# A two-layer recurrent trunk on one core: the SSD mixer's decays summed in PSUM, and a unit's preparation placed behind the unit before it

## The chip, the core and the metric

The kernel is one program on one core of a Trainium2 chip. The core has a matrix engine (TensorE; PE in the profile, with PEld for its weight loads), three engines for elementwise work (VectorE, ScalarE and GpSimd: DVE, ACT and POOL) and SyncE (SP), which issues transfers. Each engine works off its own instructions in the order in which they stand; engines wait for each other through semaphores. Matrix products are written to PSUM, eight banks of 128 x 512 float32.

The metric is the device time of the program in microseconds (us). The kernel before was timed in three runs.

## The reference, cut to what matters

A two-layer network takes 1024 prompt tokens and 8 separate decode tokens. Layer 0 is a hybrid mixer and an MLP; layer 1 is an SSD mixer and an MLP. The change is in the SSD mixer, whose core is a linear recurrence with one decay per head, evaluated in blocks of 128 tokens (chunks):

```python
def decay_linear_attention(q, k, v, g, s0, chunk):
    ...
    causal = (idx[:, None] >= idx[None, :])[None, :, :, None, None]
    def step(s, blk):
        qc, kc, vc, gc = blk
        gcum = jnp.cumsum(gc, axis=1)
        diff = gcum[:, :, None] - gcum[:, None, :]
        decay = jnp.where(causal, jnp.exp(jnp.where(causal, diff, 0.0)), 0.0)
        scores = jnp.einsum('bigk,bjgk->bijg', qc, kc)
        y_intra = jnp.einsum('bijgr,bjgrv->bigrv', scores[..., None] * decay, vc)
        y_inter = jnp.einsum('bigk,bgrkv->bigrv', qc, s) * jnp.exp(gcum)[..., None]
        g_end = gcum[:, -1]
        s_new = s * jnp.exp(g_end)[..., None, None] + jnp.einsum(
            'bjgk,bjgrv->bgrkv', kc, vc * jnp.exp(g_end[:, None] - gcum)[..., None])
        return s_new, y_intra + y_inter
```

There are 4 groups of 8 heads. `q` (C in the kernel), `k` (B) and so `scores` are shared by the 8 heads of a group; `decay`, a 128 x 128 matrix for every chunk and head, is not.

## The kernel before, in words

**Stages.** The tokens lie on the free axis (1032 columns, in three slices of 344), features on the 128 partitions. The residual stream is held as two exact float32r parts (`xh`, `xl`), weights are split likewise (`whi` by ACT on line 144, `wlo` by DVE on line 145), and each product of a projection is three matmuls of 344 columns (lines 150 to 152). A projection tile of 128 features is 72 of them, into three banks of the tag `g`.

**The SSD stage** (`ssm_mixers`) runs over the four groups. For each group `ssd_group` is a generator: it emits a piece of the recurrence and yields, and at every yield `ssm_mixers` emits one projection tile (`next(tiles)`): a tile of the next group's x, B or C with its convolution and silu (`conv_tile`, `conv_silu`; on DVE lines 1451, 409, 411, 413, 421), or a gate tile of the group before (`gate`, `gates`; lines 1476, 421, 1487). What is emitted is then put in order by a list scheduler with a timing model of its own: where it believes that TensorE would wait, it moves later projection matmuls forward. So the order on an engine differs from the order in the code, and is printed below where it matters.

**A unit** is two chunks; a group has four. In the kernel before each unit is emitted whole, then a projection tile, one or two steps of the decode recurrence (`ssd_decode`; DVE lines 1727 and 1731, POOL line 1730), and another tile. A unit is:

- preparation: x is transposed (line 1598) and scaled by dt to `xdt` (DVE, line 1600), and that to `xd2` (POOL, line 1602); B is transposed and the scores B C are made (lines 1610, 1611), then `bt` is copied (ACT, line 1612) and the causal mask put on the scores (`sc`, DVE, line 1613); for each pair of heads a bank gets the row term of the decay by two matmuls with 64 rows of contraction (line 1621, `sel` and `grow`), and ACT subtracts the column term with a Relu for each head and chunk (line 1625, 16 of 128 x 128) and takes two Exps of 128 x 1024 (line 1628); DVE multiplies one chunk's eight matrices by the scores and POOL the other's (line 1629); two more pairs of matmuls (line 1636) and two Exps (line 1637) give `EG`; ACT scales the skip term (line 1640);
- products, for each of the two chunks: `py` (line 1648, from `xdt` and `E`; added to x by DVE, line 1650), `pi` (line 1654, from the state; scaled by DVE, line 1657), and `pS` (line 1660, the new state; added by DVE, line 1666).

**PSUM.** Three banks serve the projections (`g`), three the tag `m` (`pm()`: the transposes, the scores, the decay terms, `EG`, the decode's broadcasts), two the tag `s` (`ps2()`: py, pi, pS). A matmul waits until the tile that had its bank has been read. In the trace the tiles are named `pg`, `pm` and `ps`.

Of the kernel before, what the change touches and what calls it, by code (L numbers as in the profile page):

```python
# [18 lines left out]
P = 128  # L19
T = 1032                     # 1024 prompt tokens, then 8 decode tokens  # L20
# [4 lines left out]
KT = 8                       # k-tiles of the model dimension  # L25
WN = 384                     # tokens of a group of a narrow projection
CH = 128                     # mixer chunk
# the tokens in nines of 128, the last of which overlaps
# [16 lines left out]
# order of the hybrid projection's m-tiles (first column of each)  # L45
# [14 lines left out]
# blocks of the output projections: the first packed column's k-tile, the mixer outputs  # L60
# [13 lines left out]
# columns of the retention's constants  # L74
# [9 lines left out]
class Pools:  # L84
    """A mixer's two pools: what the output projection's first block needs or reuses, and the rest."""
# [10 lines left out]
class Kern:  # L96
# [35 lines left out]
    def load_w(self, src, n, normw=None, lo_eng=None, dst=None, norm_eng=None):  # L132
        """src [128, n] of a packed weight unit -> exact float32r high and low parts."""
# [31 lines left out]
    def products(self, src, M, normw, pss):  # L165
        """The products of an m-tile over the model dimension; yields after every sixth."""
# [512 lines left out]
    def gdn_head(self, gp, h, feat, st):  # L679
# [10 lines left out]
        def bc(x, n=4):      # [128, n] -> [128, n, 128]  # L690
            return x.unsqueeze(2).to_broadcast([P, n, 128])
# [1194 lines left out]
```

## Time and profile before

| what | value |
|---|---|
| three runs | 3253.94, 3255.11, 3256.97 us |
| median | 3255.11 us |
| span of the profiled execution, first to last instruction | 3239.5 us |
| TensorE busy in the span | 3086.4 us (95%) |
| VectorE, GpSimd, ScalarE busy | 1740.3, 1241.3, 896.2 us |
| TensorE's clock over the span, share of full speed | 0.960 |

The profile gives the profiled execution's span, and no time of its own beside it; the median of the runs is 15.6 us above the span, which is what lies around it. TensorE is busy nearly always, but two things hide in that: it is busy for twice as long where its clock is at half, and a matmul's modelled end overlaps the next one's start, so that the time a matmul really takes in a stream is read from the starts. The rows below the diff show both for the stretch 1588 to 2262 us, which holds the SSD recurrence from the first unit's decay terms to the last group's products.

### The profile page before, as it was taken

The page shows a single profiled execution, that of the slowest core. Times are in us where ns is not written, and L with a number is a line of the kernel's source. Part 1 is how long each engine was busy: PE and PEld are TensorE (multiplying, and loading weights), DVE is VectorE, ACT ScalarE, POOL GpSimd, SP SyncE. Part 2 cuts the span into 40 slices and gives each one's busy share as a digit, 9 for nine tenths or more (in the row PEclk, how much of TensorE's full clock was granted, in tenths as well). Part 3 has the DMA queues.
Part 4 walks back from the last instruction along what each step waited for, and adds up shares of the span by engine and source line. Part 5 has one row for each costly group of instructions (what it writes and reads, how often), then busy time and mean ns, then how long its engine had stood idle before and what let it go on. Part 6 is the DMA issues. An engine that isn't in the chain of part 4 may idle for free. (4 is left out here: it accounts for less than half of the span.)

```text
span 3239.5 us, 49390 instructions
## 1 busy us (share of the span) xinstructions
PE 3086.4 (95%) x19566; PEld 2929.6 (90%) x19566; DVE 1740.3 (54%) x3201; ACT 896.2 (28%) x1828; POOL 1241.3 (38%) x1234
## 2 busy tenths in 40 slices
PE   7989998989999999999999999999899999999998
PEld 6888888879999999999987788887899999999998
DVE  7664667464333333337886785967635333333334
ACT  3222221223111111114444444354213111111112
POOL 4232324155333323225355555444625332332324
PEclk9899999889999999999998898998899999999999
DMA  3011103142111111111111111222431111111112
GB/s 123 20 47 54 47 26 112 55 168 64 46 46 47 49 46 46 48 48 40 55 56 58 69 62 43 82 69 79 157 140 43 46 47 49 46 46 50 46 46 72
DMA packets 102326, 202.13 MB, mean 62 GB/s; under 512 B 12624, under 2 KB 27728, under 8 KB 102096
## 3 DMA queue, kind: packets, MB, share of 16 engines
q1 hardware_dynamic: 94800, 173.82, 16.7%
q0 software_dynamic: 7296, 25.17, 2.0%
q8 instruction: 154, 2.52, 0.3%
q14 instruction: 76, 0.62, 0.1%
HBM read 157.94 MB, written 38.89 MB: 61 GB/s over the span
## 5 line engine op out<-in xcount | busy, mean ns | idle before, releaser
L150 PE MATMUL pg<-xh,whi 128*128 128x344 f32 x3072 | 1020.7, 332 | 10.2 <-DVE sxc L1451 6.5
L152 PE MATMUL pg<-xh,wlo 128*128 128x344 f32 x3072 | 1012.9, 330 | 2.8 <-DVE wlo L145 2.8
L151 PE MATMUL pg<-xl,whi 128*128 128x344 f32 x3072 | 1009.0, 328 | 0.0
L150 PEld LDWEIGHTS pg<-xh,whi 128*128 128x128 f32 x3072 | 593.0, 193 | 27.7 <-issue 8.8
L152 PEld LDWEIGHTS pg<-xh,wlo 128*128 128x128 f32 x3072 | 592.8, 193 | 12.7 <-issue 5.2
L144 ACT CAST whi<-raw 128x512 fp32r<-128x512 f32 (+2 forms) x443 | 271.0, 612 | 1191.5 <-PE pg L151 723.9
L151 PEld LDWEIGHTS pg<-xl,whi 128*128 128x128 f32 x3072 | 592.3, 193 | 8.8 <-issue 5.8
L140 POOL TENSOR_TENSOR raw<-raw,vec 128x512 f32<-128x512 f32 x264 | 300.7, 1139 | 589.9 <-DMA raw<-w 339.7
L151 PE MATMUL pg<-alo,whi 128*128 128x344 f32 (+2 forms) x1476 | 472.4, 320 | 0.0
L152 PE MATMUL pg<-ahi,wlo 128*128 128x344 f32 (+2 forms) x1476 | 472.3, 320 | 0.0
L150 PE MATMUL pg<-ahi,whi 128*128 128x344 f32 (+2 forms) x1476 | 471.6, 319 | 0.0
L1236 DVE TENSOR_TENSOR acc<-acc,pg 128x344 f32<-128x344 f32 x360 | 182.8, 511 | 385.4 <-PE pg L152 385.4
L145 POOL TENSOR_TENSOR wlo<-raw,whi 128x512 fp32r<-128x512 f32 (+2 forms) x179 | 223.7, 1251 | 327.7 <-ACT whi L144 326.6
L145 DVE TENSOR_TENSOR wlo<-raw,whi 128x512 fp32r<-128x512 f32 x264 | 209.6, 794 | 193.3 <-ACT whi L144 172.2
L1227 POOL TENSOR_TENSOR r<-r 128x344 f32<-128x344 f32 x192 | 145.9, 760 | 387.6 <-ACT ahi L1226 338.5
L152 PEld LDWEIGHTS pg<-ahi,wlo 128*128 128x128 f32 x1476 | 277.6, 188 | 0.0
L150 PEld LDWEIGHTS pg<-ahi,whi 128*128 128x128 f32 x1476 | 277.5, 188 | 0.0
L151 PEld LDWEIGHTS pg<-alo,whi 128*128 128x128 f32 x1476 | 277.3, 188 | 0.0
L1228 DVE TENSOR_TENSOR alo<-r,ahi 128x344 fp32r<-128x344 f32 x192 | 135.6, 707 | 253.8 <-POOL r L1227 253.8
L1226 ACT ACTIVATE ahi<-r 128x344 fp32r<-128x344 f32 x192 | 94.5, 492 | 338.5 <-DVE r L1225 338.5
L1225 DVE SCALAR_TENSOR_TENSOR r<-pg,rstd_bc 128x344 f32<-128x344 f32 x186 | 94.8, 510 | 76.9 <-PE pg L152 75.6
L150 PE MATMUL pg<-mhi,whi 128*128 128x344 f32 x408 | 131.3, 322 | 4.1 <-DVE acc L1342 4.1
(534 smaller groups left out, 4422.9 us busy)
## 6 DMA issues: line engine op xcount, KB each, us to landing
raw<-w SPq DMA_DIRECT2D x256, 256.0 KB, 2.6
raw<-wis SPq DMA_DIRECT2D x80, 256.0 KB, 2.6
raw<-wih SPq DMA_DIRECT2D x56, 256.0 KB, 2.6
mraw<-spill SPq DMA_DIRECT2D x17, 512.0 KB, 4.1
accd<-ost SPq DMA_DIRECT2D x48, 172.0 KB, 2.1
acc<-accd SPq DMA_DIRECT2D x16, 516.0 KB, 6.9
dS<-sstate SPq DMA_DIRECT2D x32, 256.0 KB, 3.5
o_sssm<-dS POOLq DMA_DIRECT2D x32, 256.0 KB, 2.4
```

The source lines that it names most:

```text
L140: (norm_eng or nc.gpsimd).tensor_tensor(out=r3, in0=r3, in1=normw.unsqueeze(2).to_broadcast([P, k, n // k]), op=ALU.mult)
L144: nc.scalar.copy(hi[:, :n], raw[:, :n])
L145: (lo_eng or nc.vector).tensor_tensor(out=lo[:, :n], in0=raw[:, :n], in1=hi[:, :n].bitcast(F32), op=ALU.subtract)
L150: t.matmul(ps, lhsT=whi, rhs=xhi, start=start, stop=False)
L151: t.matmul(ps, lhsT=whi, rhs=xlo, start=False, stop=False)
L152: t.matmul(ps, lhsT=wlo, rhs=xhi, start=False, stop=stop)
L1225: nc.vector.scalar_tensor_tensor(out=r, in0=ps, scalar=0.0, in1=self.rstd_bc[:, s], op0=ALU.max, op1=ALU.mult)
L1226: nc.scalar.activation(hi[:, s], r, AF.Square)
L1227: nc.gpsimd.tensor_tensor(out=r, in0=r, in1=r, op=ALU.mult)
L1228: nc.vector.tensor_tensor(out=lo[:, s], in0=r, in1=hi[:, s].bitcast(F32), op=ALU.subtract)
L1236: nc.vector.tensor_tensor(out=s, in0=s, in1=ps, op=ALU.add)
```

## The change

The decay matrices of two heads and both chunks of a unit are now built in one PSUM bank by five matmuls: the causal mask (a 128 x 128 matrix of 0 and -1e30 through an identity, 512 columns), the row term of each head (256 columns) and, for each chunk, minus the column term of both heads (256 columns, the moving operand a broadcast of `nsel`). One Exp of 128 x 512 then reads the bank. The 16 Relus and two Exps of a unit become four Exps, and the mask is no longer put on the scores: `bt` and `sc` become one copy `sb` on ACT. `E` is split by heads rather than by chunks, so that both chunks' products read both of its tiles. `grow`, `sel` and `selg` get 128 partitions (the upper 64 rows of `grow` are zero), so these matmuls contract over 128 rows in place of 64.

The preparation becomes a function. That of the first unit is emitted ahead of a yield of its own (ten yields for a group where there were nine), and that of unit u + 1 directly behind unit u's products, ahead of the next projection tile.

```diff
-        grow = gp.tile([64, SEQ], F32R, tag="row", name="sgrow", bufs=1)
+        grow = gp.tile([P, SEQ], F32R, tag="row", name="sgrow", bufs=1)
+        nc.vector.tensor_scalar(out=grow[64:].rearrange("p (c k) -> p c k", c=8), in0=self.U[64:].unsqueeze(1).to_broadcast([64, 8, 128]),
+                                scalar1=0.0, scalar2=None, op0=ALU.mult)
...
+        idr = gp.tile([P, P], F32R, name="sidr")
+        nc.vector.tensor_copy(idr, self.ident)
+        mmr = gp.tile([P, P], F32R, name="smmr")
+        nc.vector.tensor_copy(mmr, self.minmask)
+        nsel = gp.tile([P, 32], F32R, name="snsel")
+        nc.vector.tensor_scalar(out=nsel, in0=sel.bitcast(F32), scalar1=-1.0, scalar2=None, op0=ALU.mult)
...
-        for u in range(4):
+        def prepare(u):
...
+            E = [gp.tile([P, 4, 2, 128], F32, tag="E", name="E", bufs=2) for k in range(2)]
+            for hp in range(4):
+                h = g * 8 + hp * 2
+                pG = self.pm()
+                p4 = pG.rearrange("p (h c k) -> p h c k", h=2, c=2)
+                t.matmul(p4, lhsT=st["idr"], rhs=st["mmr"].unsqueeze(1).unsqueeze(1).to_broadcast([P, 2, 2, 128]), start=True, stop=False)
+                for k in range(2):
+                    t.matmul(p4[:, k], lhsT=st["sel"][:, h + k:h + k + 1].to_broadcast([P, P]),
+                             rhs=grow[:, ucols].rearrange("p (c k) -> p c k", c=2), start=False, stop=False)
+                for j in range(2):
+                    t.matmul(p4[:, :, j], lhsT=grow[:, (c0 + j) * 128:(c0 + j + 1) * 128],
+                             rhs=st["nsel"][:, h:h + 2].unsqueeze(2).to_broadcast([P, 2, 128]), start=False, stop=j == 1)
+                a.activation(E[hp // 2][:, hp % 2 * 2:hp % 2 * 2 + 2], p4, AF.Exp)
...
+            a.copy(sb, pt.rearrange("p (c k) -> p c k", c=4))
...
-            a.copy(bt, pt[:, 0:256].rearrange("p (c k) -> p c k", c=2))
-            v.tensor_tensor(out=sc, in0=pt[:, 256:512].rearrange("p (c k) -> p c k", c=2),
-                            in1=self.U.unsqueeze(1).to_broadcast([P, 2, 128]), op=ALU.mult)
...
-                        a.activation(E[j][:, hp * 2 + k, :], pG[:, k * 256 + j * 128:k * 256 + j * 128 + 128], AF.Relu,
-                                     scale=-1.0, bias=st["gc"][:, c0 + j, h:h + 1])
-            for j in range(2):
-                a.activation(E[j], E[j], AF.Exp, scale=-1.0)
-                (gs if j else v).tensor_tensor(out=E[j], in0=E[j], in1=sc[:, j, :].unsqueeze(1).to_broadcast([P, 8, 128]), op=ALU.mult)
+            for k in range(2):
+                (gs if k else v).tensor_tensor(out=E[k], in0=E[k], in1=sb[:, 2:4].unsqueeze(1).to_broadcast([P, 4, 2, 128]), op=ALU.mult)
...
+        unit = prepare(0)
+        yield
+        for u in range(4):
+            c0 = u * 2
+            E, sb, xdt, xd2, EG = unit
...
+            if u < 3:
+                unit = prepare(u + 1)
             yield
```

The rest of the diff takes comments away and changes no instruction.

**The order on TensorE** at the start of the second unit of the first group, as the kernel before has it: a projection tile ends (`pg`), the unit's x is transposed (line 1598), then B (1610) and the scores (1611), then come the decay terms (1621) with the next tile's projection between them.

```order
L152 MATMUL pg<-xh_78,wlo 128x344
L1598 MATMUL pm<-c_67,x 128x128 x8
L1610 MATMUL pm<-c_67,bc 128x128
L1611 MATMUL pm<-bc 128x128
L1610 MATMUL pm<-c_67,bc 128x128
L1611 MATMUL pm<-bc 128x128
L1621 MATMUL pm<-sgrow,ssel 128x256 x2
L150 MATMUL pg<-xh_71,whi 128x344
L151 MATMUL pg<-xl_79,whi 128x344
L1621 MATMUL pm<-sgrow,ssel 128x256 x2
```

In the changed kernel the same tile's end is followed by the unit's first products (1665 py, 1671 pi, 1677 pS) and the decay terms of the unit after it: 1609 the mask, 1611 the rows, 1614 the columns.

```order
L152 MATMUL pg<-xh_78,wlo 128x344
L1665 MATMUL ps<-E,xdt 64x128 x8
L1671 MATMUL ps<-bc,S 128x128 x4
L1609 MATMUL pm<-smmr,sidr 128x512
L1611 MATMUL pm<-sgrow,ssel 128x256
L1677 MATMUL ps<-xd_15432,sb 128x512
L1611 MATMUL pm<-sgrow,ssel 128x256
L1614 MATMUL pm<-snsel,sgrow 128x2x128 x2
L1609 MATMUL pm<-smmr,sidr 128x512
L1611 MATMUL pm<-sgrow,ssel 128x256 x2
L1614 MATMUL pm<-snsel,sgrow 128x2x128 x2
L1609 MATMUL pm<-smmr,sidr 128x512
```

Before, 38 projection matmuls of the next tile stood between the tile's end and the first products; now none does. Behind the rows shown come the rest of the third group of decay terms, 20 projection matmuls, the second chunk's products, the fourth group, the transposes, the scores and `EG`, and then 49 projection matmuls.

**The order on VectorE** at the same place, before: the tile's evictions (1451), the unit's `xdt` (1600) around the convolution's first row (409), the convolution (411, 413), and only then the masked scores (1613).

```order
L1451 TENSOR_TENSOR sxc<-pg,rstd_bc 128x344 x2
L1600 TENSOR_TENSOR xdt<-pm,dt 128x512
L409 TENSOR_SCALAR x<-sxc,scwh 128x8
L1600 TENSOR_TENSOR xdt<-pm,dt 128x512
L411 SCALAR_TENSOR_TENSOR x<-sxc,scwh,x 128x1024
L413 SCALAR_TENSOR_TENSOR x<-sst,scwh,x 128x8
L411 SCALAR_TENSOR_TENSOR x<-sxc,scwh,x 128x1024
L413 SCALAR_TENSOR_TENSOR x<-sst,scwh,x 128x8
L411 SCALAR_TENSOR_TENSOR x<-sxc,scwh,x 128x1024
L413 SCALAR_TENSOR_TENSOR x<-sst,scwh,x 128x8
L1613 TENSOR_TENSOR sc<-pm,c_67 128x256
```

In the changed kernel the same convolution stands between the readings of two product banks: py's (1667) and pi's (1674), with the decode's reductions (1750) ahead of it and a silu (421) behind.

```order
L409 TENSOR_SCALAR x<-sxc,scwh 128x8
L1667 TENSOR_TENSOR x<-x,ps 128x4x128
L1750 TENSOR_REDUCE dy<-dpr 128x4 x2
L411 SCALAR_TENSOR_TENSOR x<-sxc,scwh,x 128x1024
L413 SCALAR_TENSOR_TENSOR x<-sst,scwh,x 128x8
L411 SCALAR_TENSOR_TENSOR x<-sxc,scwh,x 128x1024
L413 SCALAR_TENSOR_TENSOR x<-sst,scwh,x 128x8
L411 SCALAR_TENSOR_TENSOR x<-sxc,scwh,x 128x1024
L413 SCALAR_TENSOR_TENSOR x<-sst,scwh,x 128x8
L1674 TENSOR_TENSOR yi<-ps,EG 128x512
L421 SCALAR_TENSOR_TENSOR x<-th,x 128x516
L1683 TENSOR_TENSOR S<-S,ps 128x512
```

So the convolution moved from behind the readers of the `m` banks to between the readers of the two `s` banks.

## Rows read from the trace of the kernel before

**Rows 1.** The windows view of the SSD stretch and of a stretch in the first MLP: length, then busy time (and instructions) of each engine, then the granted clock of TensorE as a share of full speed, the DMA share and GB/s.

```profile
1588.00:2262.00 674.00, 628.35 (x3751) 551.48 (x3750) 510.27 (x799) 310.42 (x721) 337.22 (x296) 0.91 0.19 64
1000.00:1100.00 100.00, 100.00 (x639) 100.00 (x638) 35.95 (x63) 17.95 (x32) 31.43 (x32) 1.00 0.16 48
```

**Rows 2.** TensorE's waits in the stretch 1588 to 2262 us, by line and by who ended them: us in total, times, the longest.

```profile
PE pm L1621 <- DVE xdt L1600: 14.0, 8, 3.0
PE pm L1621 <- DVE sc L1613: 13.0, 5, 3.4
PE pg L150 <- DVE sxc L1451: 6.5, 4, 2.7
PE pg L152 <- DVE wlo L145: 2.6, 3, 1.7
PE ps L1648 <- DVE x L1650: 2.2, 3, 1.0
PE pm L1636 <- ACT E L1625: 1.9, 2, 0.9
PE ps L1660 <- DVE x L1650: 1.7, 3, 0.7
PE pg L150 <- ACT whi L144: 1.3, 2, 0.7
PE ps L1654 <- DVE S L1666: 1.2, 3, 0.8
```

**Rows 3.** The timeline around one such wait, TensorE and then VectorE: start, us, the instruction with its count, and in brackets the idle time before it and who ended it.

```profile
1635.81 1.03 PE L1598 MATMUL pm<-c,x 128*128 128x128 f32 x8
...
1637.12 0.39 PE L1611 MATMUL pm<-bc 128*128 128x128 f32 x2
1640.23 0.50 PE L1621 MATMUL pm<-sgrow,ssel 64*128 64x256 f32 x2 [2.73 <-DVE xdt L1600]
...
1636.36 1.78 DVE L145 TENSOR_TENSOR wlo<-raw,whi 128x512 fp32r<-128x512 f32 x1
1638.06 0.67 DVE L1731 TENSOR_REDUCE dy<-dpr 128x4 f32<-128x512 f32 x1
...
1639.51 0.68 DVE L1600 TENSOR_TENSOR xdt<-pm,dt 128x512 f32<-128x512 f32 x1
```

**Rows 4.** The windows view around another of these waits, 2.2 us long and ended at 1713.8 us; the columns are those of rows 1.

```profile
1710.00:1714.00 4.00, 1.80 (x12) 1.55 (x11) 4.00 (x7) 1.25 (x2) 0.48 (x3) 0.96 0.13 37
1714.00:1730.00 16.00, 16.00 (x51) 13.40 (x52) 6.88 (x15) 9.46 (x24) 7.77 (x6) 0.50 0.11 35
1730.00:1741.00 11.00, 10.25 (x81) 8.10 (x79) 8.62 (x16) 1.98 (x5) 5.62 (x6) 0.97 0.06 25
```

**Rows 5.** TensorE's timeline where one pair of line 1621 stands between projection matmuls at full clock.

```profile
1590.10 0.32 PE L151 MATMUL pg<-xl,whi 128*128 128x344 f32 x1
1590.35 0.49 PE L1621 MATMUL pm<-sgrow,ssel 64*128 64x256 f32 x2
1590.78 0.43 PE L152 MATMUL pg<-xh,wlo 128*128 128x344 f32 x1
1591.04 0.32 PE L150 MATMUL pg<-xh,whi 128*128 128x344 f32 x1
```

**Rows 6.** ScalarE's groups in the stretch 1588 to 2262 us: busy us, mean ns of one, idle before and who ended it.

```profile
L1625 ACT ACTIVATE E<-pm,sgc 128x128 f32<-128x128 f32 x256 | 71.8, 373 | 59.1 <-PE pm L1621 58.9
...
L1628 ACT ACTIVATE E<-E 128x1024 f32<-128x1024 f32 x32 | 32.8, 1081 | 0.0
...
L1637 ACT ACTIVATE EG<-pm 128x512 f32<-128x512 f32 x32 | 18.0, 622 | 0.0
```

**Rows 7.** VectorE's groups in the same stretch, in the same columns.

```profile
L145 DVE TENSOR_TENSOR wlo<-raw,whi 128x512 fp32r<-128x512 f32 x64 | 65.8, 1029 | 12.9 <-PE pg L152 11.8 <-ACT whi L144 0.9
L411 DVE SCALAR_TENSOR_TENSOR x<-sxc,scwh,x 128x1024 f32<-128x1024 f32 x36 | 52.1, 1446 | 4.0 <-ACT x L408 3.8
...
L421 DVE SCALAR_TENSOR_TENSOR x<-th,x 128x516 f32<-128x516 f32 x24 | 23.3, 970 | 2.8 <-ACT th L420 2.8
...
L421 DVE SCALAR_TENSOR_TENSOR z<-th,z 128x516 f32<-128x516 f32 x28 | 22.4, 801 | 10.8 <-ACT th L420 10.8
L1629 DVE TENSOR_TENSOR E<-E,sc 128x1024 f32<-128x1024 f32 x16 | 21.9, 1370 | 15.8 <-ACT E L1628 15.8
L1650 DVE TENSOR_TENSOR x<-x,ps 128x512 f32<-128x512 f32 x32 | 21.8, 683 | 27.5 <-PE ps L1648 27.5
...
L1731 DVE TENSOR_REDUCE dy<-dpr 128x4 f32<-128x512 f32 x31 | 21.0, 676 | 4.1 <-POOL dpr L1730 4.1
...
L413 DVE SCALAR_TENSOR_TENSOR x<-sst,scwh,x 128x8 f32<-128x8 f32 x36 | 13.3, 370 | 0.3
```

**Rows 8.** TensorE's timeline over a chunk's products: py (two passes of eight), pi (two of four), pS (two of one), and the next projection matmul.

```profile
1605.89 1.09 PE L1648 MATMUL ps<-E,xdt 128*64 128x128 f32 x16 [0.60 <-DVE x L1650]
1606.91 1.16 PE L1654 MATMUL ps<-bc,S 128*128 128x128 f32 x8
1607.91 1.02 PE L1660 MATMUL ps<-xd,bt 128*128 128x512 f32 x2
1608.37 0.72 PE L152 MATMUL pg<-xh,wlo 128*128 128x344 f32 x1
```

**Rows 9.** VectorE's groups, in the columns of rows 7, in the stretch 1000 to 1100 us of the first MLP, the weights' low parts.

```profile
L145 DVE TENSOR_TENSOR wlo<-raw,whi 128x512 fp32r<-128x512 f32 x9 | 6.2, 690 | 13.7 <-ACT whi L144 13.4
```

More of the change, by code (lines that the diff above doesn't have):

```diff
@@ L1428, in ssm_setup @@
                 nc.tensor.transpose(pt[:64, j * 128:(j + 1) * 128], ghl[:, half * 4 + j, :], self.ident)
-            nc.scalar.copy(grow[:, half * 512:half * 512 + 512], pt[:64, :])
-        sel = gp.tile([64, 32], F32R, name="ssel")
-        nc.vector.tensor_tensor(out=sel, in0=self.ident[:64, 0:32], in1=self.ident[:64, 32:64], op=ALU.add)
+            nc.scalar.copy(grow[:64, half * 512:half * 512 + 512], pt[:64, :])
+        sel = gp.tile([P, 32], F32R, name="ssel")
+        nc.vector.tensor_tensor(out=sel, in0=self.ident[:, 0:32], in1=self.ident[:, 32:64], op=ALU.add)
+        idr = gp.tile([P, P], F32R, name="sidr")
[4 more added lines that the diff above has]
+        nc.vector.tensor_scalar(out=nsel, in0=sel.bitcast(F32), scalar1=-1.0, scalar2=None, op0=ALU.mult)
         pt = self.pm()
@@ L1437, in ssm_setup @@
         nc.scalar.copy(dg, pt[:32, 0:16])
-        st.update(dt=dt, gc=gc, kdf=kdf, egend=egend, grow=grow, sel=sel, sel8=sel8, dg=dg)
+        st.update(dt=dt, gc=gc, kdf=kdf, egend=egend, grow=grow, sel=sel, nsel=nsel, idr=idr, mmr=mmr, sel8=sel8, dg=dg)
         return st
@@ L1582, in v64 @@
             return ap.rearrange("p (h k) -> p h k", h=8)
-        selg = gp.tile([64, 8, 64], F32R, tag="selg", name="selg", bufs=1)
-        v.tensor_copy(selg, st["sel"][:, hs].bitcast(F32).unsqueeze(2).to_broadcast([64, 8, 64]))
+        selg = gp.tile([P, 8, 64], F32R, tag="selg", name="selg", bufs=1)
+        v.tensor_copy(selg, st["sel"][:, hs].bitcast(F32).unsqueeze(2).to_broadcast([P, 8, 64]))
         selg = selg.rearrange("p h k -> p (h k)")
         dec = self.ssd_decode(gp, g, x, B, C, st, half, selg)
-        S = None
-        for u in range(4):
+        grow = st["grow"]
+        def prepare(u):
             c0 = u * 2
             ucols = slice(c0 * 128, c0 * 128 + 256)
+            E = [gp.tile([P, 4, 2, 128], F32, tag="E", name="E", bufs=2) for k in range(2)]
[11 more added lines that the diff above has]
+                a.activation(E[hp // 2][:, hp % 2 * 2:hp % 2 * 2 + 2], p4, AF.Exp)
+            pt = self.pm()
+            sb = gp.tile([P, 4, 128], F32, tag="sb", name="sb", bufs=1)
+            for j in range(2):
+                cc = slice((c0 + j) * 128, (c0 + j + 1) * 128)
+                t.transpose(pt[:, j * 128:(j + 1) * 128], B[:, cc], ident)
+                t.matmul(pt[:, 256 + j * 128:256 + (j + 1) * 128], lhsT=B[:, cc], rhs=C[:, cc], start=True, stop=True)
+            a.copy(sb, pt.rearrange("p (c k) -> p c k", c=4))
             xdt, xd2 = [], []
@@ L1635, in ssd_group @@
                     i = hp * 2 + k
-                    t.matmul(pG[:, k * 256:k * 256 + 256], lhsT=selg[:, i * 128:i * 128 + 128], rhs=st["grow"][:, ucols], start=True, stop=True)
+                    t.matmul(pG[:, k * 256:k * 256 + 256], lhsT=selg[:, i * 128:i * 128 + 128], rhs=grow[:, ucols], start=True, stop=True)
                 a.activation(EG[:, hp * 2:hp * 2 + 2, :], pG.rearrange("p (i k) -> p i k", i=2), AF.Exp)
@@ L1640, in ssd_group @@
                 a.activation(x[:, i, ucols], x[:, i, ucols], AF.Copy, scale=self.V("sd", g * 4 + i))
+            return E, sb, xdt, xd2, EG
+        S = None
+        unit = prepare(0)
[3 more added lines that the diff above has]
+            E, sb, xdt, xd2, EG = unit
             for j in range(2):
@@ L1647, in ssd_group @@
                         h = i * 2 + k
-                        t.matmul(py[k * 64:k * 64 + 64, i * 128:(i + 1) * 128], lhsT=xdt[j][:, h * 64:h * 64 + 64], rhs=E[j][:, h, :], start=True, stop=True)
+                        t.matmul(py[k * 64:k * 64 + 64, i * 128:(i + 1) * 128], lhsT=xdt[j][:, h * 64:h * 64 + 64], rhs=E[h // 4][:, h % 4, j, :], start=True, stop=True)
                 xv = x[:, :, cc]
@@ L1659, in ssd_group @@
                 pS = self.ps2()
-                t.matmul(pS, lhsT=bt[:, j, :], rhs=xd2[j], start=True, stop=True)
+                t.matmul(pS, lhsT=sb[:, j, :], rhs=xd2[j], start=True, stop=True)
                 Sn = gp.tile([P, 512], F32, tag="S", name="S", bufs=2)
```

16 lines of the change are left out of this document (removed).

## The prediction

> **What bounds the kernel now.** I read the windows view first, for the SSD stretch and for a quiet one beside it [rows 1]. The SSD stretch is 674 us long. TensorE is busy for 628.35 of them, so it waits for 45.65. Its granted clock there is 0.91 of full speed, against 1.00 in the MLP, so (1 - 0.91) x 674 = 60.7 us of array time are lost by running at half clock. No other engine comes near the length: VectorE has 510, GpSimd 337, ScalarE 310. The stretch is TensorE's, and at most 45.65 + 60.7 = 106 us of it are not work.
>
> The waits view says where the waits are [rows 2]. Line 1621, the decay rows, has 14.0 + 13.0 = 27.0 us in 13 waits; line 1636 has 1.9. The products (1648, 1660, 1654) have 2.2 + 1.7 + 1.2 = 5.1. Projections waiting for evictions or weights have 6.5 + 2.6 + 1.3 = 10.4, which the change does not address. The timeline shows what such a wait is [rows 3]: x and the scores are on their way at 1635.8 and the last of these matmuls starts at 1637.12, but the reader `xdt` starts only at 1639.51, since VectorE is late with a weight split (1.78 us), a reduction and evictions. The next `pm` bank is not free, and TensorE stands for 2.73 us. What follows a wait of that length is the dearer part [rows 4]: after the 2.2 us wait before 1714 us the clock is 0.50 for 16 us, the lower of its two levels (1.2 of 2.4 GHz), though TensorE is never idle in them. I put the 60.7 us down to the 13 waits of line 1621: 4.7 us of lost array time for each. The drop in rows 4 alone cost 8, so this is a mean over some that cost little.
>
> **The change, part by part.**
>
> *Array work.* In the MLP 639 matmuls of 344 columns start in 100 us [rows 1]: 156.5 ns each, or 0.455 ns a column. A pair of line 1621 between projections takes from 1590.10 to 1591.04 with two projection matmuls in it [rows 5]: 0.94 - 2 x 0.157 = 0.63 us, where 512 columns would be 0.233. The other 0.39 are spent on entering and leaving the form with 64 rows. By the order before there are 56 runs of line 1621 (64 pairs) and 29 of line 1636 (32 pairs). That is 85 x 0.63 + 11 x 0.233 = 56.1 us. After the change there are 64 groups of 512 + 4 x 256 = 1536 columns, 0.699 us each, 44.7 us, and 32 pairs for `EG` of 0.233, 7.5 us, all with 128 rows: 52.2 us. So the mask and the column terms triple the columns and yet the work falls by **3.9 us**. The moving operand with step 0 of the column terms is in no row. Its price lies between nothing, the same columns as elsewhere, and 64 x (0.63 - 0.233) = 25 us, if each of the 64 pairs cost as much as one of line 1621. I take nothing, since rows 5 has the same step on the weights and the time there goes to the change of form; the 25 us stay in the range.
>
> The Trainium skill ("TensorE: Matmul & The Clock Gate", Back-to-back issue gap) gives 216 ns for 512 columns and about 109 for 256. By that a group would be 652 ns, an estimate, and the work would fall by 7 us in place of 3.9. The row above is the measured stream of this kernel, and I stay with it.
>
> *ScalarE.* A unit's 16 Relus and two Exps, 16 x 0.373 + 2 x 1.081 = 8.1 us, become four Exps of 128 x 512, 4 x 0.622 = 2.5 us [rows 6]. ScalarE's load falls by 16 x 5.6 = 90 us, and is not on the path: it is busy for 310 of 674 us. It counts only through TensorE: line 1636 loses its 1.9 us of waiting for `E`. The first Exp of a unit must now wait until the second chunk's py has read `E`, and the weight copies and tanhs behind it on ScalarE wait with it. That is hidden where projection matmuls already have their weights, at the price of the wait for py counted below.
>
> *VectorE, GpSimd, DMA.* VectorE loses `sc`; the products with the scores, the state and the decode stay as they are, on both engines. No DMA is added or moved past another. The setup's additional casts and the zeros of `grow` are five VectorE operations once; the largest has 1024 columns, like a convolution tap of 1.45 us [rows 7]. The first group's projections stand around them; I take nothing, and 3 us if they lie bare.
>
> *Waits.* The 27.0 us of line 1621 go: its banks are now freed by an Exp, not by VectorE. But VectorE is no earlier, and what is late next is the products. They now follow directly on a projection tile, with two `ps` banks that VectorE frees, while the tile's convolution is due. I walked the second unit of the first group by the order printed ahead, from py's start at 0. VectorE has an eviction, a weight split of 1.03 [rows 7] and a small row, so it adds py to x from 2.2 to 2.9; then two reductions (1.35), three taps and three small rows (3 x 1.446 + 3 x 0.370 = 5.45), and it reads pi from 9.7 to 10.4. TensorE does py and pi (1.02 + 1.00, [rows 8]) and 0.35 of decay terms, and waits for py's bank from 2.4 to 2.9. Then pS, the other decay terms and 20 projections (0.46 + 1.75 + 3.13) bring it to 8.3, and the second py waits for pi's bank until 10.4. With about 0.6 more for the state and for `EG` that is **3.2 us**. Where a gate tile precedes, only a silu (0.80) and reductions stand between, and the same walk gives 0.5 + 0.75 = **1.25 us**. Eight of the 16 units have a convolution, or weight splits or decode rows of like length, between their readers. So I get 8 x 3.2 + 8 x 1.25 = 35.6 us of new waits, for 27.0 + 1.9 + 5.1 = 34.0 that they replace: **+1.6 us**.
>
> *Clock.* What changes is how many waits are long. Before there were 13 on line 1621; in my walk eight units have one of about 2 us, and the other waits are under 1. At 4.7 us each, 37.6 of the 60.7 us stay: **-23.1 us**.
>
> Sum: -3.9 + 1.6 - 23.1 = -25.4 us. Against the profiled execution that is a span of 3239.5 - 25.4 = 3214.1; what lies around the span (15.6 us to the median) is not touched, so 3255.1 - 25.4 = **3229.7, say 3230 us**.
>
> **The rivals.**
>
> *A, short waits everywhere.* The new decay terms (2.8 us a unit) cover VectorE's work better than my walk says, because the convolution's taps themselves wait for ScalarE (3.8 us, [rows 7]), which has 90 us less to do. Then all 16 units are like the light ones: 20.0 us of waits in place of 34.0, and long waits only where projections wait for evictions, four of them [rows 2], 4 x 4.7 = 18.8 of clock loss. That is -3.9 - 14.0 - 41.9 = -59.8: 3195 us; if all the lost clock came back, 3177. For it: 13 of the 17 `pm` and `pg` waits on VectorE's evictions are on a line that no longer needs VectorE. Against it: the same VectorE with the same work behind the same tile.
>
> *B, the lateness just moves.* In rows 3 VectorE was late by more than its queue's mean durations say. The weight split's mean is 1029 ns in this stretch and 690 in the MLP [rows 7, 9], beside a GpSimd busy for half the time. If that meets 12 of 16 units rather than 8, waits are 12 x 3.2 + 4 x 1.25 = 43.4 (+9.4), clock loss is 12 x 4.7 = 56.4 (-4.3), and with the array's -3.9 the sum is +1.2: 3256 us, no change. The Trainium skill ("GPSIMD Engine Reference", 1. Specifications) says that GpSimd shares its SBUF interfaces with VectorE, with contention for instructions of two SBUF inputs. The trace's 1029 against 690 agrees, and the change takes no such work from GpSimd; by the rule alone this rival would be the forecast.
>
> *C, slower.* A unit is now one block without projections to fill it: products twice (2 x 2.48, [rows 8]), decay terms 2.8, `EG` 0.47, transposes and scores about 1.5 [rows 3], 9.7 us. If the first wait in it drops the clock and the clock stays down through the block, 9.7 us are lost in each. In rows 4 it stayed down for 16 us in which drains and projections alternated. With 10 such blocks 97 us would be lost in place of 60.7, and the sum is 36.3 - 3.9 + 1.6 = +34: 3289 us. It decides from (60.7 + 2.3) / 9.7 = 6.5 blocks on. Against it: in rows 4 the clock was back at 0.97 while products and transposes ran (1730 to 1741).
>
> **How the numbers follow.** The forecast gets 0.39 (own range 3212 to 3248), A 0.26, B 0.17, C 0.18. I trust the mechanism (line 1621's waits must go) more than the size. The range reaches down to 3178, nearly the whole clock loss of A, and up to 3275, which takes in the 25 us of the column terms on B and the lower half of C; some 0.08 lies below and 0.11 above. A measurement of this kernel tells apart about 0.2%, 6.5 us. Faster by more: the forecast and A, 0.65. Within: B, 0.16. Slower: C and a little of B, 0.19.
>
> **What would show it.** Right: no wait of the decay terms for `xdt` or the scores; the waits view led by py, pi or pS waiting for VectorE's `x`, `yi` or `S`, 30 to 40 us; a mean clock of about 0.94 in the stretch; a group of decay terms in 0.7 us. A is right if these waits are near 20 us and the clock is 0.97; B if they are over 43 us and the clock is still 0.91; C if the clock is below 0.88 and low while products run. The step on the column terms is wrong if a pair of them takes much over 0.25 us at full clock. The whole is wrong if the time changes outside the SSD stretch.

## The result and the profile after

| what | kernel before | changed kernel |
|---|---|---|
| median of 4 runs each, on one chip | 3254.53 us (3253.21 to 3256.97) | 3209.62 us (3203.04 to 3227.82) |
| ratio, 95% interval | 1 | 0.987 [0.9839, 0.9901] |
| span of the profiled execution | 3239.5 us | 3200.8 us |

The changed kernel is 45 us faster, 1.0 to 1.6%. Predicted were 25 us.

The two profiles are compared over one and the same piece of work: from the first matmul of the first unit's preparation to the norm of the last group. This reaches some 45 us further than the stretch of [rows 1], since a fixed end time would cut off different work in the two. The windows view gives for it, in the columns of [rows 1], before:

```profile
1588.96:2307.27 718.31, 663.22 (x3930) 584.56 (x3928) 549.17 (x845) 325.71 (x740) 366.92 (x315) 0.90 0.20 70
```

and after:

```profile
1600.93:2271.58 670.65, 620.94 (x4122) 567.39 (x4121) 531.63 (x829) 268.76 (x516) 386.39 (x315) 0.98 0.23 75
```

The stretch is 47.7 us shorter, TensorE is busy for 42 us less of it although it has 192 more matmuls, and its mean granted clock has risen from 0.90 to 0.98. Behind the stretch little changed: 3239.5 - 2307.27 = 932.2 us before, 3200.8 - 2271.58 = 929.2 after. Ahead of it the layer whose code the change does not touch took 12 us longer in this execution, which is taken up under the eighth run below.

TensorE's waits in the stretch after (us in total, times, the longest), which answer to [rows 2]:

```profile
PE ps L1677 <- DVE x L1667: 10.6, 10, 2.2
PE ps L1665 <- DVE yi L1674: 9.8, 6, 3.0
PE pm L1645 <- DVE selg L1594: 5.2, 1, 5.2
PE pg L150 <- DVE sxc L1460: 4.8, 4, 1.9
PE pg L150 <- DVE z L1485: 4.5, 2, 2.5
...
PE pm L1609 <- ACT E L1616: 2.1, 2, 1.2
PE ps L1665 <- DVE S L1683: 1.9, 2, 1.0
PE pm L1609 <- DVE xdt L1632: 1.9, 1, 1.9
PE pm L1645 <- DVE xdt L1632: 1.7, 4, 0.6
...
PE ps L1665 <- DVE x L1667: 0.8, 2, 0.4
```

Of the 27.0 us of the decay rows waiting for `xdt` and `sc`, one wait of 1.9 us is left (1609, for `xdt`). In their place the products wait for VectorE's readers of the two `s` banks: pS for `x`, py for `yi`, `S` and `x`, 10.6 + 9.8 + 1.9 + 0.8 = 23.1 us. The preparation has 5.2 + 2.1 + 1.9 + 1.7 = 10.9 us of its own. So TensorE waits nearly as long as before; the gain is elsewhere.

TensorE's timeline after, at two places: `EG`'s pairs between projection matmuls, and decay terms directly behind a state product:

```profile
1681.86 0.50 PE L1645 MATMUL pm<-sgrow,selg 128*128 128x256 f32 x2
1682.20 0.32 PE L151 MATMUL pg<-xl,whi 128*128 128x344 f32 x1
1682.40 0.51 PE L1645 MATMUL pm<-sgrow,selg 128*128 128x256 f32 x2
1682.74 0.32 PE L152 MATMUL pg<-xh,wlo 128*128 128x344 f32 x1
...
1982.74 0.80 PE L1611 MATMUL pm<-sgrow,ssel 128*128 128x256 f32 x2
1983.38 0.38 PE L1614 MATMUL pm<-snsel,sgrow 128*128 128x256 f32 x2
1983.60 0.40 PE L1609 MATMUL pm<-smmr,sidr 128*128 128x512 f32 x1
1983.84 0.40 PE L1611 MATMUL pm<-sgrow,ssel 128*128 128x256 f32 x2
1984.07 0.38 PE L1614 MATMUL pm<-snsel,sgrow 128*128 128x256 f32 x2
1984.29 0.39 PE L1609 MATMUL pm<-smmr,sidr 128*128 128x512 f32 x1
```

From start to start a group is 0.24 + 0.23 + 0.22 = 0.69 us (1983.60 to 1984.29), and the column terms (1614) take 0.22 for 512 columns: their step of 0 costs nothing. But a pair at this place takes 1682.20 to 1682.74 with one projection matmul, 0.54 - 0.157 = 0.38 us, not 0.233. And the 512 columns behind a state product take 0.64 (1982.74 to 1983.38); whose time that is, the part on the prediction takes up.

**An account of the stretch.** To compare kernels, each stretch is cut in three. *Waits* are its length less TensorE's busy time. *Lost clock* is half of the time for which the trace's record of the granted clock stands at 0.5, which overstates it a little, since TensorE also waits in these pieces. *Array* is the busy time less the lost clock, the work at full speed. The three add up to the length. Each row is one profiled execution; the ratio is that of the runs. The two rows of the changed kernel differ by 1 to 2 us in each term, so a difference of that size between two rows says nothing.

| kernel | ratio to before | length | array | lost clock (pieces) | waits |
|---|---|---|---|---|---|
| before | 1 | 718.3 | 594.9 | 68.3 (14) | 55.1 |
| changed | 0.987 | 670.7 | 605.6 | 15.4 (7) | 49.7 |
| changed, run again | 0.9865 | 672.8 | 607.1 | 17.1 (9) | 48.6 |
| 1: new decays, old place | 1.0005 | 715.5 | 596.5 | 39.3 (12) | 79.8 |
| 2: before, 128 rows | 0.9875 | 678.7 | 574.1 | 34.1 (11) | 70.4 |
| 3: changed, 64 rows | 0.9931 | 689.9 | 636.8 | 20.5 (8) | 32.6 |
| 4: before, new place | 0.9926 | 684.1 | 597.3 | 39.3 (8) | 47.5 |
| 5: before, 128 rows, new place | 0.9824 | 652.1 | 572.1 | 22.2 (8) | 57.8 |
| 6: changed, no mask | 0.9879 | 669.6 | 590.4 | 20.5 (10) | 58.7 |
| 7: changed, two selg | 0.9865 | 669.6 | 604.2 | 20.5 (7) | 44.9 |
| 9: changed, pS in m | 0.9921 | 689.5 | 608.2 | 23.9 (11) | 57.4 |
| 10: 5 with pS in m | 0.9864 | 665.1 | 578.3 | 23.9 (12) | 62.9 |

From before to after: array +10.7, lost clock -52.9, waits -5.4, together -47.6. The prediction had -3.9, -23.1 and +1.6.

### The profile page after: what moved, and what is told of

Its sections match the earlier page's. It is cut to its first block, busy times and chain, and to the rows that moved or that the text cites. A ratio compares the mean times of both kernels' runs of the same rounds, so it can differ in the third digit from the quotient of the medians.

```text
span 3200.8 us, 49506 instructions
## 1 busy us (share of the span) xinstructions
PE 3052.8 (95%) x19758; PEld 2918.4 (91%) x19758; DVE 1724.0 (54%) x3189; ACT 841.2 (26%) x1604; POOL 1264.1 (39%) x1234
## 5 line engine op out<-in xcount | busy, mean ns | idle before, releaser
L150 PE MATMUL pg<-xh,whi 128*128 128x344 f32 x3072 | 1003.2, 327 | 10.8 <-DVE sxc L1460 4.8
L151 PE MATMUL pg<-xl,whi 128*128 128x344 f32 x3072 | 998.2, 325 | 0.0
L152 PE MATMUL pg<-xh,wlo 128*128 128x344 f32 x3072 | 997.2, 325 | 0.7 <-DVE wlo L145 0.7
L150 PEld LDWEIGHTS pg<-xh,whi 128*128 128x128 f32 x3072 | 585.5, 191 | 18.4 <-DVE sxc L1460 5.8
L152 PEld LDWEIGHTS pg<-xh,wlo 128*128 128x128 f32 x3072 | 585.2, 191 | 4.5 <-issue 1.7
L151 PEld LDWEIGHTS pg<-xl,whi 128*128 128x128 f32 x3072 | 584.2, 190 | 4.8 <-issue 2.8
L140 POOL TENSOR_TENSOR raw<-raw,vec 128x512 f32<-128x512 f32 x264 | 306.2, 1161 | 636.8 <-DMA raw<-w 330.0
L145 DVE TENSOR_TENSOR wlo<-raw,whi 128x512 fp32r<-128x512 f32 x264 | 198.4, 752 | 195.6 <-ACT whi L144 185.8
```

The lines of the kernel that those rows point to most:

```text
L140: (norm_eng or nc.gpsimd).tensor_tensor(out=r3, in0=r3, in1=normw.unsqueeze(2).to_broadcast([P, k, n // k]), op=ALU.mult)
L145: (lo_eng or nc.vector).tensor_tensor(out=lo[:, :n], in0=raw[:, :n], in1=hi[:, :n].bitcast(F32), op=ALU.subtract)
L150: t.matmul(ps, lhsT=whi, rhs=xhi, start=start, stop=False)
L151: t.matmul(ps, lhsT=whi, rhs=xlo, start=False, stop=False)
L152: t.matmul(ps, lhsT=wlo, rhs=xhi, start=False, stop=stop)
```

## The experiments

Two theories of the large clock term stood against each other. **The form:** the 64-row matmuls between projections cost array time and keep the clock down. **The place:** with the preparation behind the preceding unit's products the long waits are gone. The change does both, and puts the sums into PSUM as a third thing. The first four runs separate them; they share one set of runs of the kernel before, of 3255.64 us in the median.

**1. The new decays in the old place.**

```diff
-        unit = prepare(0)
-        yield
         for u in range(4):
             c0 = u * 2
-            E, sb, xdt, xd2, EG = unit
+            E, sb, xdt, xd2, EG = prepare(u)
...
-            if u < 3:
-                unit = prepare(u + 1)
             yield
```

> The decays summed in PSUM, but each unit prepared where the kernel before prepares it, ahead of its own products. Form theory (the 64-row matmuls between projections cost array time and hold the clock down; without them a dropped clock comes back at once): most of the gain is there, about 3215 us, clock in the SSD stretch 0.96 or more. Place theory (the gain comes from preparing a unit behind the products of the one before): about 3250 us, clock near the 0.90 of before.

Measured: 3259.35 us, ratio 1.0005 [0.9982, 1.0028]. The whole gain is gone, although no 64-row matmul is left. The largest of TensorE's waits in its stretch:

```profile
PE ps L1562 <- DVE z L1496: 18.9, 3, 6.3
PE pm L1609 <- ACT E L1616: 10.6, 5, 2.5
PE ps L1663 <- DVE E L1638: 8.8, 6, 1.8
PE pm L1645 <- ACT sb L1623: 7.4, 6, 1.6
PE ps L1663 <- POOL E L1638: 6.6, 4, 2.0
PE ps L1663 <- DVE xdt L1632: 6.2, 2, 3.1
```

Emitted whole, the unit has its Exps, the product with the scores and `xdt` directly ahead of py: 8.8 + 6.6 + 6.2 = 21.6 us of py waiting for them, and 18.0 more of the preparation waiting for ScalarE. The longest, 18.9 us, is no part of a unit: the matmul of a group's norm (1562) waits for VectorE's sum of squares (`z`). Neither theory gave this: the time is nearer to the place theory's, but the low clock falls, from 136.5 us before to 78.5, and waits take back what it gives. Experiment 2 has the same rows in the same place without the sums, and is faster by 42 us by the ratios. The new decays depend on the new place.

**2. The kernel before with 128 rows.** Its `grow`, `sel` and `selg` get 128 partitions; everything else stays. The printed order is that of the kernel before on every engine, apart from the setup and the rows' form.

```diff
-        grow = gp.tile([64, SEQ], F32R, tag="row", name="sgrow", bufs=1)
+        grow = gp.tile([P, SEQ], F32R, tag="row", name="sgrow", bufs=1)
...
-        selg = gp.tile([64, 8, 64], F32R, tag="selg", name="selg", bufs=1)
+        selg = gp.tile([P, 8, 64], F32R, tag="selg", name="selg", bufs=1)
...
-                    t.matmul(pG[:, k * 256:k * 256 + 256], lhsT=st["sel"][:, h:h + 1].to_broadcast([64, P]), rhs=st["grow"][:, ucols], start=True, stop=True)
+                    t.matmul(pG[:, k * 256:k * 256 + 256], lhsT=st["sel"][:, h:h + 1].to_broadcast([P, P]), rhs=st["grow"][:, ucols], start=True, stop=True)
```

> The kernel before, with nothing changed but the contraction of lines 1621 and 1636: 128 rows, the upper 64 zero. Form theory: 34 us of array time (85 runs of 0.39 us) and at least 20 us of clock loss go, 3190 to 3205 us, although the waits of 1621 for xdt and sc stay. Place theory: the waits stay and with them the clock loss of about 70 us, so at most the array time goes, 3220 us or more.

Measured: 3220.33 us, ratio 0.9875 [0.9841, 0.9909]. 35 us by the medians from one part of the change, and not by fewer waits. The decay rows still wait as in [rows 2], for `xdt` and the masked scores:

```profile
PE pm L1623 <- DVE xdt L1602: 15.4, 9, 2.7
PE pm L1623 <- DVE sc L1615: 13.4, 6, 3.4
```

What changed most is how long the clock stays down after such a wait. In [rows 4] one of 2.2 us stands in the kernel before, with the clock at 0.50 for the 16 us behind it. The same wait here, 2.21 us, ended at 1729.34; the windows view around it:

```profile
1725.30:1729.30 4.00, 1.83 (x12) 1.54 (x10) 4.00 (x7) 1.23 (x2) 0.48 (x3) 1.00 0.12 37
1729.30:1732.71 3.41, 3.37 (x12) 3.40 (x13) 2.22 (x4) 1.69 (x6) 2.23 (x2) 0.50 0.47 159
1732.71:1746.71 14.00, 12.65 (x97) 10.34 (x96) 12.17 (x21) 7.59 (x19) 9.76 (x8) 1.00 0.00 1
```

The same wait in the same order cost 3.41 us of half clock, not 17. Over the stretch the clock is low for 68.3 us in 11 pieces, where it was 136.5 in 14. It is not so after every wait. Eleven waits of 2 us and more stand at the same place in both, and the low clock at them adds up to 116 us before and 65 here: shorter at seven, the same at two, longer at two (a wait of 3.35 us near 1815 in both was followed by 10.2 us before and 13.7 here). In the account: array -20.8, lost clock -34.2, waits +15.3. So the time lies at the place theory's bound of 3220, but that theory's clock loss, which was to stay with the waits, is halved.

**3. The changed kernel with 64 rows** in all but the mask. Its order on every engine is that of the changed kernel.

```diff
-                    t.matmul(p4[:, k], lhsT=st["sel"][:, h + k:h + k + 1].to_broadcast([P, P]),
-                             rhs=grow[:, ucols].rearrange("p (c k) -> p c k", c=2), start=False, stop=False)
+                    t.matmul(p4[:, k], lhsT=st["sel"][:64, h + k:h + k + 1].to_broadcast([64, P]),
+                             rhs=grow[:64, ucols].rearrange("p (c k) -> p c k", c=2), start=False, stop=False)
...
```

> The changed kernel, with the row and column terms and EG contracted over 64 rows again (the mask over 128). Form theory: about 36 us of array time come back (two changes of form for each of 64 groups at 0.39 us a run, and those of EG) and the clock falls, 3245 us or more. Place theory: the waits are as short as in the changed kernel and the clock stays at 0.97 or more, 3215 to 3225 us.

Measured: 3236.5 us, ratio 0.9931 [0.9902, 0.9961], 20 to 22 us slower than the changed kernel by the ratios, between the two expectations. The array's term is 31 us larger, 17 of them hidden in shorter waits. The clock is hardly lower: 41.0 us in 8 pieces. So 64 rows keep the clock down in the order of the kernel before, but hardly here.

**4. The kernel before in the new place**: its own decays, with 64 rows, Relus and the mask on the scores; only `prepare` and the additional yield.

```diff
-        for u in range(4):
-            c0 = u * 2
+        def prepare(u):
+            c0 = u * 2
...
+        unit = prepare(0)
+        yield
+        for u in range(4):
+            c0 = u * 2
+            E, bt, xdt, xd2, EG = unit
...
+            if u < 3:
+                unit = prepare(u + 1)
             yield
```

> The kernel before, with its own decays (64 rows, Relus, masked scores), and only the preparation moved behind the products of the unit before, with the additional yield. Form theory: no gain to speak of, 3245 to 3265 us, clock near 0.90. Place theory: most of the gain, about 3215 us, clock 0.96 or more.

Measured: 3235.52 us, ratio 0.9926 [0.99, 0.9951]: 20 us by the medians, 24 by the ratio, less than the 35 and 41 of the rows alone and between the two expectations. The pieces of low clock fall from 14 to 8, but each is as long as before: 136.5 / 14 = 9.8 us, and 78.5 / 8 = 9.8. With experiment 2 (68.3 / 11 = 6.2) this splits the clock's gain: the place makes the drops fewer, the rows make them shorter.

**5. 128 rows and the new place, without the sums in PSUM.** The edits of 2 and 4 together; TensorE's order in the stretch is that of experiment 4. This and the next three ran on one chip, against 3255.57 us before.

> The kernel before's own decays (Relus, mask on the scores, one pair of matmuls for two heads) with 128 rows of contraction, and the preparation moved behind the preceding unit's products: two parts of the change without the mask and the column terms in PSUM. Alone, the 128 rows brought 35 us and the place 20. Theory of two causes (64 rows cost array time and hold the clock down; the place takes the long waits away; the sum in PSUM is a price of its own, 64 x 1024 columns more, about 29.8 us at 0.455 ns a column): the two gains add up, 3256 - 55 = 3200 or lower, the stretch near 640 us, busy time at full clock near 575 us as with 128 rows alone, low pieces of the clock of 4 to 6 us on average rather than 9.8. Rival, the sum in PSUM is needed for the gain because the Relus' 16 ScalarE operations a unit and the longer wait for E keep TensorE standing: no faster than the changed kernel, 3210 to 3225, with 60 us or more of waits, led by py waiting for E.

Measured: **3200.91 us** (3188.04 to 3210.44, six runs), ratio 0.9824 [0.9795, 0.9852], the fastest kernel of this study. The changed kernel on the same chip had 3215.06 (3210.43 to 3220.04, five runs). The first theory's sum was met: the clock is low in pieces of 44.4 / 8 = 5.5 us, the array's term is 572.1. The stretch is 12 us longer than the 640 that it gave, by waits, and the rival's waits for `E` did not come:

```profile
PE ps L1669 <- POOL dpr L1741: 11.0, 2, 5.7
PE pg L150 <- DVE z L1478: 10.2, 2, 9.1
PE ps L1657 <- DVE yi L1666: 10.0, 5, 3.7
PE ps L1657 <- DVE x L1659: 5.0, 3, 2.5
```

The mask and the column terms in PSUM cost the changed kernel 33.5 us of array and give back 15 in waits and clock: the kernel without them, with the Relus on ScalarE, is 14 us faster in the medians.

**6. The changed kernel without the mask's matmul.** It leaves the causal mask out and takes the exponents at a thousandth, so that they stay finite.

```diff
-    t.matmul(p4, lhsT=st["idr"], rhs=st["mmr"].unsqueeze(1).unsqueeze(1).to_broadcast([P, 2, 2, 128]), start=True, stop=False)
...
-    a.activation(E[hp // 2][:, hp % 2 * 2:hp % 2 * 2 + 2], p4, AF.Exp)
+    a.activation(E[hp // 2][:, hp % 2 * 2:hp % 2 * 2 + 2], p4, AF.Exp, scale=0.001)
```

> The changed kernel without the mask's matmul (the causal mask is left out, and the exponents are taken at a thousandth so that they stay finite): 64 matmuls of 512 columns less. If columns count by their stream alone, 64 x 0.233 = 14.9 us less than the changed kernel, busy time in the stretch near 606, about 3195. If these matmuls stand where TensorE would wait for py's or pi's bank anyway, the waits grow by what the array saves and the time falls by less than 7 us.

Measured: 3218.76 us, ratio 0.9879 [0.9853, 0.9905], no faster than the changed kernel. The array's term falls by 15.2 us, the 14.9 of the columns, and the waits grow by 9.0 and the lost clock by 5.1. TensorE's waits, where new ones stand for the work that is gone:

```profile
PE ps L1664 <- DVE yi L1673: 8.4, 5, 2.8
PE ps L1676 <- DVE x L1666: 8.4, 3, 4.8
PE pm L1644 <- DVE xdt L1631: 7.0, 4, 3.4
...
PE pm L1620 <- ACT E L1615: 4.0, 3, 2.8
```

The second expectation holds in the time: what the array saves is lost to waits and clock. Its reason, that TensorE would wait at these places anyway, is not shown, since the order changed too: at 792 of the 4056 places that are left in the stretch, a matmul of another kind stands than in the changed kernel.

**7. Two buffers for selg** in the changed kernel, with the cumulative decays' tile among the half tiles to make room.

```diff
-        gc = gp.tile([P, 8, 32], F32, name="sgc")
+        gc = gp.tile([P, 8, 32], F32, tag="hf", name="sgc", bufs=SHF)
...
-        selg = gp.tile([P, 8, 64], F32R, tag="selg", name="selg", bufs=1)
+        selg = gp.tile([P, 8, 64], F32R, tag="selg", name="selg", bufs=2)
```

> The changed kernel with two buffers for selg (the cumulative decays' tile takes its place among the half tiles). If the one wait of 5.2 us on selg's cast is the buffer's, it goes, and with it one drop of the clock: 5 to 8 us less than the changed kernel. If the cast is late because VectorE gets to it late, nothing changes: within 3 us.

Measured: 3217.06 us, ratio 0.9865 [0.9835, 0.9895]. The wait of 5.2 us is gone from the trace, so it was the buffer's, as the first expectation had it, but the time is the same: against the changed kernel's second run the waits fell by 3.7 us and the clock lost 3.4 more.

**8. The changed kernel again**, unedited.

> The changed kernel itself, unedited, so that the three others can be compared with it on the same chip: 3210 us, within 10, and 0.987 of the kernel before. If the 12 us by which its profiled layer 0 was longer than the kernel before's belong to that execution and not to the change, layer 0 here is 1589 to 1616 us long as in the other profiles, and the SSD stretch is again 671 us, within 5.

Measured: 3215.06 us, ratio 0.9865 [0.9837, 0.9893]. The stretch is 672.8 us long, 2.2 more than in the first profile. Layer 0, the same instructions in all kernels, is shown by the windows view from the start to the stretch, in the kernel before:

```profile
0.00:1588.96 1588.96, 1512.56 (x9878) 1438.21 (x9879) 831.16 (x1704) 384.57 (x750) 552.21 (x602) 0.97 0.19 59
```

in the changed kernel's first profile:

```profile
0.00:1600.93 1600.93, 1524.30 (x9878) 1447.52 (x9879) 833.30 (x1708) 385.80 (x750) 554.93 (x602) 0.96 0.19 59
```

and in its second:

```profile
0.00:1615.53 1615.53, 1541.02 (x9879) 1462.77 (x9879) 835.04 (x1708) 384.94 (x750) 551.64 (x602) 0.95 0.18 58
```

The same kernel differs from itself by 14.6 us here, with the granted clock at 0.96 and 0.95, and in the profiles of the other experiments this part took 1608.5 to 1617.2. So a difference of these 12 us comes from execution to execution and needs no change of the kernel. A difference of spans between two single profiles of this program carries an error of that size; a difference over the same stretch carries less.

**9 and 10. The state's product in a bank of m**, in the changed kernel and in the kernel of experiment 5. This tries the readers of the two `s` banks, the longest waits that are left. They ran on one chip, against 3257.95 us before.

```diff
-                pS = self.ps2()
+                pS = self.pm()
```

> The changed kernel with the state's product pS in a bank of the tag m in place of s: the two s banks then hold py and pi alone. In the changed kernel pS waits 10.6 us for py's reader and py 9.8 us for pi's. If the two s banks that VectorE frees late are what bounds the changed kernel, the 10.6 us go and with them one or two of its drops of the clock: 8 to 15 us faster than it, about 3203. If VectorE's lateness only moves (the m banks are now three for four users, and the decay terms wait behind VectorE's addition of the state): within 5 us of it, with waits of the decay terms for the state's reader in place of pS's.

Measured: 3234.01 us, ratio 0.9921 [0.9898, 0.9944], 18 us slower than the changed kernel's second run by the ratios. pS no longer leads the waits; `pi` does, for the state itself:

```profile
PE ps L1671 <- DVE S L1683: 14.7, 8, 3.2
```

> The kernel before's own decays with 128 rows, at the new place, and the state's product in a bank of the tag m. Without the last of these it took 3201 us, with 14.6 us of waits of py's and pS's matmuls for VectorE's and GpSimd's readers and 11.0 of pS behind a decode product. If the s banks are the bound, these 11 to 20 us go: 3180 to 3190. If the lateness moves: 3195 to 3205.

Measured: 3213.3 us, ratio 0.9864 [0.9834, 0.9895], 13 us slower than experiment 5 by the ratios. Here py and pi wait 9.1 + 7.1 + 5.3 us for VectorE's `S` and `x`:

```profile
PE pg L152 <- DVE wlo L145: 10.9, 9, 3.9
PE ps L1663 <- DVE S L1675: 9.1, 5, 2.6
PE ps L1657 <- DVE x L1659: 7.1, 2, 3.6
PE ps L1663 <- DVE S L1672: 5.3, 3, 2.1
```

Neither expectation gave a loss. In these two orders the bank was not the bound: without pS in the `s` banks, the products wait for VectorE's result instead of its reading. But the scheduler changed the order besides, and a matmul of another kind stands at 880 of 4056 places of the stretch in 9 and at 1636 of 3928 in 10. How much of the 13 to 18 us is the bank's and how much the order's was not separated.

## Why the prediction was right in its direction and too small

**The mechanism held, and the term that was mis-sized most was the clock.** The decay rows' waits went, and products waiting for VectorE came in their place. The prediction kept eight long waits at 4.7 us of lost clock each, -23.1 us in all. There were seven drops, close to eight, but a drop cost 15.4 / 7 = 2.2 us. The step that failed is the one that put "the 60.7 us down to the 13 waits of line 1621" as a price of a wait: it took the length of a drop for a property of the wait. Experiment 2 shows that it is not: with the waits in place and 128 rows in the matmuls, half of the low clock goes. The prediction counted 128 rows as array work alone, and did not see a second effect on the clock, 34.2 us there. Experiment 4 shows the other half: with the rows as before, the place takes six of 14 drops away and leaves the price of one at 9.8 / 2 = 4.9 us, close to the 4.7 that were predicted. The three terms missed by -29.8 us (clock), -7.0 (waits) and +14.6 (array). That the time came within 20 us of the forecast is in part luck: the array's error, of the other sign, hid half of the clock's.

**Array work: -3.9 predicted, +10.7 measured.** In the account's steps, the place adds 2.4 us (before to experiment 4), 128 rows take 25.2 away (4 to 5), and the sums add 33.5 (5 to the changed kernel). A group of decay terms was right to 0.01 us (0.69 for 0.699) and the step of 0 in its operand was rightly taken as nothing. What a run of the 64-row form costs was right as well, at full clock. The next pair behind [rows 5], before and in experiment 2:

```profile
1591.35 0.31 PE L152 MATMUL pg<-xh,wlo 128*128 128x344 f32 x1
1591.60 0.50 PE L1621 MATMUL pm<-sgrow,ssel 64*128 64x256 f32 x2
1592.02 0.42 PE L150 MATMUL pg<-xh,whi 128*128 128x344 f32 x1
1592.28 0.32 PE L151 MATMUL pg<-xl,whi 128*128 128x344 f32 x1
...
1612.34 0.32 PE L152 MATMUL pg<-xh,wlo 128*128 128x344 f32 x1
1612.50 0.40 PE L1623 MATMUL pm<-sgrow,ssel 128*128 128x256 f32 x2
1612.73 0.32 PE L150 MATMUL pg<-xh,whi 128*128 128x344 f32 x1
1612.89 0.32 PE L151 MATMUL pg<-xl,whi 128*128 128x344 f32 x1
```

With its two projection matmuls the pair takes 0.93 us with 64 rows and 0.55 with 128, no more than its columns. Over the 34 pairs between projections that run at full clock and without a wait in both kernels, the medians are 0.94 and 0.55: 0.39 a run (0.37 to 0.40 at 29 of them, 0.20 to 0.22 at the five others, of which the pair of [rows 5] is one). The prediction took this for all 85 runs, 33.7 us; it measured 20.8 (before to experiment 2, 83 runs in the trace), 25.2 (experiment 4 to 5, 81 runs) and 31.3 (experiment 3 to the changed kernel, 107 runs), 0.25 to 0.31 us a run. Behind a wait only about 0.19 is saved, and a run at half clock in both saves 0.59, of which the account counts half. The Trainium skill ("TensorEngine Tiling (Array Packing)", Key Properties) says that a change of tiling mode drains TensorE; the rows agree with a cost there, 0.39 us for entering and leaving.

Two more prices were missed. `EG`'s pairs in the changed order take 0.38 us in the rows shown, where 0.233 was taken. And the sums cost 33.5 us where 64 x 1024 columns were 29.8; in the old place (experiment 2 to 1) they cost 22.4, so their price hangs on the order, and what makes it was not separated. The 0.64 us behind a state product do not explain it. A projection matmul there takes as much more; in the kernel before, the one at 1608.37 in [rows 8] is followed by

```profile
1608.92 0.32 PE L150 MATMUL pg<-xh,whi 128*128 128x344 f32 x1
```

that is after 0.55 us in place of 0.157. The 0.40 us belong to the state product, whose last matmul starts 0.03 us ahead, and the walk, which gave the product 0.46, had it too short.

**Waits: +1.6 predicted, -5.4 measured.** Waits that replace the 34.0 us of line 1621, line 1636 and the products were walked as 35.6 us; in the profile they are 23.1 of the products and 10.9 of the preparation, 34.0. The sum is close, the places are not: the walk knew neither selg's wait nor those for ScalarE's `E` and for `xdt`, and put their time on the products. The 5 us are from waits that the change was not to touch, such as those for the weights' low parts (2.6 us in [rows 2], and none after).

**The small steps.** ScalarE's load fell by 325.7 - 268.8 = 57 us, not by 90, and stayed off the path. Part of the 90 was a misreading: Relus overlap, and [rows 6] has the 256 of them busy for 71.8 us, not for 256 x 0.373 = 95.5. The time around the span was taken as 15.6 us, as the distance from a profile's span to a median of other executions. The run that was profiled after took 3203.04 us for a span of 3200.8, so 2.2 us lie around the span and the rest was the difference of two executions. It did no harm, since only the difference was added to the median.

**The rivals.** By the signs set down ahead, A (3195) came nearer than the forecast: the waits of py, pi and pS for VectorE are 23.1 us, where A has near 20 and the forecast 30 to 40, and the clock is 0.98, where they have 0.97 and 0.94. But A's reason, short waits everywhere, is not what the runs show: with the preparation's 10.9 us the waits that replace the old ones are 34, not 20, and the clock came back by shorter drops. The time lies between the forecast and A. B, the lateness that only moves, is true of the waits alone, and the gain did not need them. Of C nothing came: the clock is not low through a unit's block.

**What would have proved the whole wrong** was a change outside the SSD stretch. The 12 us of layer 0 look like one, and the second profile shows that they are not the change's.

**What stays open.** That 128 rows nearly halve the low clock is shown in two orders, that of the kernel before (136.5 to 68.3 us) and that of experiment 4 (78.5 to 44.4 in experiment 5), in one profile each. Why they did so little in the changed order (41.0 to 30.7 us, experiment 3, where a drop costs 2.6 us even with 64 rows), and what sets the length of a single piece, no run here separates.

## What to carry to other kernels

When a change has several parts, price each one alone on the same order before believing the sum: here 128 rows of contraction, three tile sizes, brought as much as the whole rewrite, and the rewrite without its sums in PSUM beats both. Lost clock is a price of the wait and of what runs behind it: ask of every short matmul of another form between long ones not only what it costs but how long the engine stays slow around it. A matmul that is taken away, or a buffer that is added, need not gain anything: here the next wait, or another order, took it back.

## What the runs showed that I had not expected

- A wait of 2.2 us was followed by 17.06 us at 1.2 GHz with 64-row pairs among the projections, and by 3.41 us with 128-row pairs in the same order.
- The matmul behind a state product, a projection or a decay term alike, took 0.40 us more than elsewhere from its start to the next one's.
- 64 matmuls of 512 columns taken away (15.2 us of array), with the order that came of it, changed the time by less than the runs' spread.
- Layer 0, the same instructions, took 1589 to 1617 us in the twelve profiled executions of this study, at mean granted clocks of 0.95 to 0.97.
